# Tile 5 of the stick-breaking heads turned by VectorE and DRAM, with a newly planned instruction order

## The chip, the cores and the metric

The kernel runs on one core of a Trainium2 chip. The metric is device time in microseconds (us), the median of the runs shown, lower is better. PE is TensorE (matmul), PEld its weight load, DVE VectorE, ACT ScalarE, POOL GpSimd, SP SyncE, whose queue issues all DMA transfers.

## What is computed

One layer of a streaming encoder, for a prompt of 1024 rows and a sample of 32 rows, model width 1024, all in float32. Two groups of eight heads of 64 share one input projection: A is band attention with a clipped position bias, B is stick-breaking attention.

```python
qa, ka, va, ga, qb, kb, vb, gb = split(rmsnorm(h, g_pre) @ w_in)        # 8 x 512 columns

# A: each 64-row chunk reads itself and the 8 chunks before it
w = softmax(where(ok, qa @ ka.T * HEAD_DIM**-0.5 + bias[clip(k - q)], -1e30)); oa = w @ va

# B: strictly causal
z = qb @ kb.T * HEAD_DIM**-0.5
log_1m = where(causal, log_sigmoid(-z), 0)
after = cumsum(log_1m, reverse=True) - log_1m
w = where(causal, exp(log_sigmoid(z) + after), 0); ob = w @ vb

y = concat(oa * silu(ga), ob * silu(gb)) @ w_out
h = h + rmsnorm(y, g_post)
h = h + sigmoid(h @ w_ple_gate) * (p @ w_ple)
```

The keys and values are outputs too. The sample rows attend to cached keys and values.

## The kernel before

**Split operands.** Every float32 operand of a product is split in a rounded high part and the remainder, and three (or two) products of the parts are summed. So each turned tile costs a copy (high part, ACT) and a subtraction (low part, mostly DVE).

**The attention stages.** There are eight stages n = 0 to 7, for the head pairs A0, B0, A1, B1, A2, B2, A3, B3; each has two heads. While PE works on the scores and values of stage n, the projections of the pair of stage n + 1 are woven between (24 matmuls of 352 columns for each of three chunks and each of q, k, v); in the last stage these are the gates. A head has eight query tiles i of 128 rows. For each tile:

- `scores(i)`: score matmuls into up to two of three PSUM banks `S`. For B: DVE adds the mask on the diagonal block, ACT makes two sigmoids (of -z into `om`, of z into `be`), DVE's scan multiplies up from the right in `om`, POOL multiplies `be` by `om`. Tile i has i + 1 blocks of 128 columns in B, at most five in A.
- `weights_t(i)`: turns the weights, since the value product needs keys on the partitions. The usual way is by PE: transposes by 128x128 block into one of two PSUM banks `ptw`, four blocks to a bank, then ACT copies to `wTh` and DVE subtracts into `wTl`.
- `values(g)`: for each half g (tiles 0 to 3, 4 to 7) value matmuls into `PV`, ACT and DVE combine its halves, and a transfer stores `ot` to `o_dr`.

`om` and `be` are rings of 3076 and 3640 columns; a tile's room is taken again after its last use. A stage is followed by the next without a barrier.

**The way past PE.** Tiles named in `ROUND` go another way: A's tile 5, and B's tiles 4 and 6. Each group of `ROUND` goes by itself:

```python
for x, _, _ in done_with:
    y = slice(first[x], first[x] + cost(x))
    nc.vector.transpose(squares[:, y], w1[:, y.start * P:y.stop * P])
dr = scratch([P, m * P], f"swap{nm}_{i}")
dma(dr, w0[:, 0:m * P])
for c in range(4):
    x = dr[:, c * m * 32:(c + 1) * m * 32].rearrange("(g k) x -> k g x", k=32)
    dma(w1[32 * c:32 * c + 32].rearrange("k (g x) -> k g x", g=4), x)
```

DVE turns each 32x32 square in place of the block (from `be` to `om`), one transfer writes `om` to DRAM (`swapB`), four read it back with the squares in their turned places (to `be`), and then ACT copies to `wTh` and DVE subtracts into `wTl`, both from `be`.

**The order.** The program records all operations (one line, L490, issues them all, so rows of the profile are told apart by tile names), and `order()` lists them by a plan: a queue for each engine, durations from `cost()`, and a key by which the waiting operations of an engine are ranked. The key is the place of recording, plus an offset by engine and name of the written tile (`AHEAD_OF`). `RATES`, `SPACE_S`, `SPACE_T`, `SPACE_V`, `SUMS_STEP` and `SAMPLE_AT` set how attention, projections, the sums of weights and the sample's attention are woven when recorded. On the chip each engine runs its list in this order and waits on semaphores.

**After the attention.** The output product and the gate product (`o0P` to `o3P`, `g0P` to `g3P`) are by Strassen's seven products for blocks of 128 rows; tile 8, the sample, goes by itself. Rows of the hidden state (`h`) are normed, x is added by POOL, and they are stored to `h_dr`; the gate reads them back, turned by DVE (`lg`, `ug` from `ht`). Blocks of the gate's weights (`gB`, `gT`) are split meanwhile. `uu` is the gate's running sum.

Of the kernel before, what the change touches and what calls it, by code (L numbers as in the profile page):

```python
# [8 lines left out]
F32 = mybir.dt.float32  # L9
# [16 lines left out]
SCALE = HD ** -0.5  # L26
NT = 9
AHEAD_OF = {
    ('ACT', 'L'): 100, ('ACT', 'Qfs'): 50, ('ACT', 'stq'): 400, ('ACT', 'x'): -50,
# [3 lines left out]
}  # L33

ROUND = {"A": ((5,),), "B": ((4,),(6,))}
LAG_T = 2
LAG_V = 2
SPACE_S = {'A': 0.1, 'B': 0}  # L40
SPACE_T = {'A': 0.4, 'B': 0.4}
SPACE_V = {'A': 0.05, 'B': 0.0}
PARTS = 4
BEHIND = 2
RATES = (0.96, 0.86, 0.92, 1.0, 1.0, 0.86, 1.12, 0.86)
PLE_LAG = 4.0


# [224 lines left out]
class Recorder:  # L273


    def __init__(self):
        self.with_table, self.old_table = [], []
        self.ops, self.cls, self.low, self.closed, self.turns = [], 0, 0, [], []
        self.tensor = Engine(self, "PE", "tensor")
        self.vector = Engine(self, "DVE", "vector")  # L280
        self.scalar = Engine(self, "ACT", "scalar")
        self.gpsimd = Engine(self, "POOL", "gpsimd")
        self.sync = Engine(self, "SP", "sync")
# [26 lines left out]
    def node(self, eng, what, args, kw, after):  # L310
        o = Op()
        o.eng, o.what, o.args, o.kw, o.after = eng, what, args, kw, after
        o.key = (self.cls if eng == "PE" else self.low, len(self.ops))
        o.shared, o.table = False, None
        self.ops.append(o)
        return o

    def add(self, eng, what, args, kw):
        writes, reads = [], []
        method = what[1] if isinstance(what, tuple) else ""  # L320
        for i, a in enumerate(args):
            if isinstance(a, (View, Raw, Segments)):
                (writes if i == 0 or (method == "tensor_tensor_reduce" and i == 7) else reads).append(a)
        for k, a in kw.items():
            if isinstance(a, (View, Raw, Segments)):
                (writes if k in ("out", "accum_out") else reads).append(a)
        o = self.node(eng, what, args, kw, set())
        for mine, write in ((reads, False), (writes, True)):
            for v in mine:
                b = v.buf  # L330
                hit = False
                for other, box, wrote in b.uses:
                    if other is not o and (write or wrote) and all(p < y and x < q for (p, q), (x, y) in zip(v.box, box)):
                        o.after.add(other)
                        hit = True
                if b.pool is not None:
                    if not hit:
                        o.after.add(b.place)
                    b.pool.ops.append(o)
                b.uses.append((o, v.box, write))  # L340
        if method == "activation" and args[2] in (AF.Exp, AF.Sigmoid):

            o.table = args[2]
            if self.with_table and self.with_table[-1].table != o.table:
                self.old_table, self.with_table = self.with_table, []
            self.with_table.append(o)
            o.after.update(self.old_table)
        if eng != "PE" and writes:
            name = str(writes[0].buf.name)
            kind = (eng, name[:next((i for i, x in enumerate(name) if x.isdigit() or x in "AB_"), len(name))])  # L350
            o.key = (o.key[0], o.key[1] + AHEAD_OF.get(kind, 0))
        o.busy, o.late = self.cost(eng, method, args, kw, writes, reads)
        if eng == "SP":
            o.pieces = max(self.pieces(v) for v in args[0:2])
        o.shared = eng == "POOL"
        if eng == "DVE":
            sbuf = [v for v in reads if isinstance(v, (View, Segments)) and not v.buf.psum and v.free() > 4]
            o.shared = len(sbuf) > 1 or (method == "tensor_copy" and len(sbuf) == 1 and not writes[0].buf.psum)
# [9 lines left out]
    @staticmethod  # L368
    def cost(eng, method, args, kw, writes, reads):

        out = writes[0] if writes else None
        n = out.free() if isinstance(out, View) else 1
        psum = any(isinstance(v, (View, Segments)) and v.buf.psum for v in reads)
        if eng == "PE":
            if method == "transpose":
                return (109 if args[1].shape[0] > 64 else 62), 165
            return max(109.0, 2.5 + 0.449 * args[2].free()) * (1 if args[2].buf.dtype == F32R else 4), 165
        if eng == "ACT":
            return (165 if psum else 200) + 0.83 * n + (190 if "accum_out" in kw else 0), 0
        if eng == "DVE":  # L380
            if method == "tensor_tensor_scan":
                return 155 + 2.08 * n, 0
            if method == "tensor_copy" and not psum:
                return 155 + 0.53 * n, 0
            if method == "scalar_tensor_tensor":
                return 210 + 1.04 * n, 0
            return 155 + 1.04 * n + (83 if method == "tensor_tensor_reduce" else 0), 0
        if eng == "POOL":
            if method == "tensor_tensor":
                if n == 1:  # L390
                    return 400, 0
                return 190 + (1.77 if out.buf.dtype == F32 else 2.15) * n, 0
            if method == "tensor_scalar":
                return 255 + 0.86 * n, 0
            return 100 + 0.82 * n, 0
        size, run = 4, 0
        for v in (out, args[1]):
            if isinstance(v, View) and v.buf.pool is not None:
                size, run = 4 * v.shape[0] * v.free(), 4 * v.shape[-1]
        return ISSUE, max(size / DMA_RATE, size / run * (8.5 + 0.0365 * run) / 16)  # L400
# [95 lines left out]
def stream_step(  # L496
# [6 lines left out]
    rec = Recorder()  # L503
# [12 lines left out]
    def scratch(shape, name):  # L516
# [28 lines left out]
        out=maskb, in_=maskb, pattern=[[-1, P]], base=0, channel_multiplier=1,  # L545
# [4 lines left out]
    ksS = const.tile([P, 4, NS], F32, tag="ksS", name="ksS")  # L550
# [735 lines left out]
    for n in range(-1, 8):  # L1286
        a = len(order)
        if n < 7:
            ab, p = pairs[n + 1]
# [120 lines left out]
                sub(b[key], b["B11"], b[key], ALU.subtract)  # L1410
                dma(sum_dr[w][kt, 3], b[key])

    SUMS_STEP = {2: [8, 34], 4: [10, 28], 5: [8, 28], 6: [14, 28]}

    def with_sums(n, att, todo):
        out = list(att)
# [1 line left out]
            out.insert(SUMS_STEP[n][i], (0.0, lambda w=w, kt=kt: sum_weights(w, kt), None))  # L1418
        return out

    SAMPLE_AT = {2: [0, 10, 16, 23, 26, 27], 3: [4, 10, 15, 22, 27, 32], 6: [1, 10, 15, 22, 27, 32], 7: [1, 9, 15, 22, 23, 32]}

    def with_sample(n, att, steps):
        out = list(att)
# [15 lines left out]
    ple = Ple(True)  # L1440
# [56 lines left out]

    seq = attention_stream()
    for n in range(8):
        den = []  # L1500
        for j in range(*span[n + 1]):
            den += col_steps(j)
        att = seq[n, 0] + seq[n, 1]
        if pairs[n][1] % 2 == 1:
            att = with_sample(n, att, sample_attention(pairs[n][0], pairs[n][1] // 2))
        att = with_sums(n, att, SUMS_AT.get(n, ()))
        weave(n, att, den)
# [2 lines left out]


    rec.close(at_stack, at)
    fb = rec.pool(ctx, tc, name="fb", bufs=1)
    GP = fb.tile([P, D], F32, tag="GP", name="GP")
    L, R = HALF
# [17 lines left out]
    ple = Ple(False)  # L1533
# [62 lines left out]
    def fetch_T(src, dst, t):  # L1596

        if src is og_dr:
            for k0 in (0, 4):
                dma(dst[:, k0:k0 + 4, :], rows_T(og_dr, k0, t))  # L1600
            return
        t0, n = rows_of(t)


        h = fa.tile([P, D], F32, tag="hh", name=f"ht{t}", bufs=2)
        dma(h[:, 0:8 * n], h1_dr[t].rearrange("b (k g) c -> (b k) (g c)", k=32))
        squares = h[:, 0:8 * n].rearrange("p (g j m) -> p g m j", j=32, m=8)
        nc.vector.transpose(dst.rearrange("p m (k g) -> p g m k", k=32), squares)


    class Side:
# [187 lines left out]

    for m, (nm, src, group) in enumerate(sets):  # L1800
        last_set = m == len(sets) - 1
        state = [{}, {}]
        for n, prod in enumerate(ORDER):
            for pair, t in enumerate(group):
# [32 lines left out]
                for c, bank in zip(pieces, banks):  # L1837
                    multiply(bank[:, c], left, b, c)
                    if nm == "g" and prod == "P3":
                        uu = st["uu"]  # L1840
# [29 lines left out]
                else:  # L1870
                    uu = st.get("uu")
                    if prod in ("P2", "P4") and pair == 0:
                        name = f"cc{m}{prod}"
                        if m == 2 and prod == "P4":
                            cc = at2.tile([P, 2, 512], F32, tag="stg", name=name, bufs=3)
                        elif m == 3 and prod == "P2":
                            cc = at0.tile([P, 2, 512], F32, tag="L0", name=name)
# [78 lines left out]
```

## Time and profile before

| | |
|---|---|
| runs | 783.26, 783.63, 783.88 us; median 783.63 |
| profiled execution | 783.64 us, span 781.9 us |
| granted TensorE clock | 0.999 |
| busy, us | PE 769.8, PEld 711.2, DVE 602.9, ACT 528.4, POOL 471.7 |
| DMA | 154.71 MB, mean 198 GB/s |

A row of a group reads: line, engine, operation, written tile <- read tiles, shapes, count | busy us in all, mean ns of one | idle us of the engine before them, and what ended it. A busy PE is not PE at its peak: matmuls overlap, and their ends are modelled.

### The profile page before, as it was taken

To read this page: it belongs to the slowest core of one execution; us is meant where nothing else is said; L and a number is where in the kernel's file an instruction comes from. 1 tells how busy PE (TensorE), PEld (TensorE's weight loads), DVE (VectorE), ACT (ScalarE), POOL (GpSimd) and SP (SyncE) were. 2 spreads that over 40 slices of the span, in tenths; PEclk is the share of its full clock that TensorE was granted. 3 is DMA by queue.
4 is the path that set the end of the run, shared out by engine and by line. 5 is a ranking of instruction groups with operands and counts; after the bars stand their busy time and mean duration, and the time that the engine had idled before them with its cause. 6 is when DMAs were issued, how large, how long until landed. Compare 5 with 4: busy or idle time off the path is not lost.

```text
span 781.9 us, 14437 instructions
## 1 busy us (share of the span) xinstructions
PE 769.8 (98%) x4534; PEld 711.2 (91%) x4534; DVE 602.9 (77%) x1127; ACT 528.4 (68%) x1146; POOL 471.7 (60%) x551
## 2 busy tenths in 40 slices
PE   8999999999999999999999999999999999999997
PEld 6999999999999999999999999999998877877786
DVE  7827767888778888688988798888474687988965
ACT  5647775877786777787767777674347867685651
POOL 5636624574666446775966677575553438599533
PEclk9999999999999999999999999999999999999999
DMA  8657634557765638776757977775689856659754
GB/s 301 215 152 180 161 82 139 136 128 210 177 196 167 183 92 240 185 213 210 197 143 199 260 209 218 197 223 167 184 276 289 274 181 220 239 160 346 250 181 134
DMA packets 184542, 154.71 MB, mean 198 GB/s; under 512 B 64705, under 2 KB 150505, under 8 KB 184466
## 3 DMA queue, kind: packets, MB, share of 16 engines
q1 hardware_dynamic: 184466, 153.79, 66.8%
q8 instruction: 36, 0.59, 0.3%
q14 instruction: 40, 0.33, 0.1%
HBM read 94.97 MB, written 50.36 MB: 186 GB/s over the span
## 4 chain that ended last, share of the span: by engine, by line
PE 80%; POOL 7%; DVE 4%; DMA 3%; issue 3%; SPq 2%; ACT 1%; POOLq 0%; DVEq 0%; ACTq 0%
PE mm_gB L490 6%; PE mm_qB L490 6%; PE mm_qA L490 5%; PE mm_vA L490 5%; PE mm_kA L490 5%; PE mm_vB L490 5%; PE mm_kB L490 4%; PE PVB L490 4%; PE SB L490 4%; PE PVA L490 3%; PE SA L490 3%; PE ptwA L490 3%; PE o1P L490 3%; PE g2P L490 2%; PE o0P L490 2%
## 5 line engine op out<-in xcount | busy, mean ns | idle before, releaser
L490 POOL TENSOR_TENSOR be<-be,om 128x256 f32<-128x256 f32 (+8 forms) x66 | 83.5, 1269 | 82.1 <-DVE om L490 48.9
L490 DVE TENSOR_TENSOR_SCAN om<-om,SB 128x384 f32<-128x384 f32 (+5 forms) x96 | 92.6, 968 | 20.2 <-ACT be L490 11.1
L490 ACT ACTIVATE om<-SB 128x384 f32<-128x384 f32 (+5 forms) x96 | 46.6, 499 | 23.8 <-DVE SB L490 12.5
L490 POOL TENSOR_SCALAR be<-be,statA 128x640 f32<-128x640 f32 (+4 forms) x64 | 46.0, 727 | 25.8 <-DVE statA L490 22.2
L490 ACT ACTIVATE be<-SB 128x384 f32<-128x384 f32 (+5 forms) x96 | 46.3, 500 | 13.2 <-DVE om L490 6.6
L490 ACT ACTIVATE be<-om,statA 128x640 f32<-128x640 f32 (+4 forms) x64 | 44.4, 695 | 5.9 <-DVE statA L490 3.9
L490 DVE TENSOR_TENSOR wTl<-ptwA,wTh 128x512 fp32r<-128x512 f32 (+2 forms) x80 | 37.2, 482 | 12.5 <-ACT wTh L490 11.4
L490 ACT CAST wTh<-ptwA 128x512 fp32r<-128x512 f32 (+2 forms) x80 | 32.2, 425 | 20.4 <-PE ptwA L490 19.1
L490 ACT CAST wTh<-ptwB 128x512 fp32r<-128x512 f32 (+3 forms) x64 | 29.8, 488 | 15.4 <-PE ptwB L490 10.7
L490 DVE TENSOR_TENSOR wTl<-ptwB,wTh 128x512 fp32r<-128x512 f32 (+3 forms) x64 | 33.5, 542 | 5.3 <-ACT wTh L490 4.9
L490 PE MATMUL SB<-kdB,LB 128*128 128x384 f32 (+5 forms) x96 | 33.4, 353 | 0.4 <-DVE om L490 0.3
L490 PE MATMUL ptwA<-ident,be 128*128 128x128 f32 x200 | 33.2, 273 | 0.0
L490 DVE CUSTOM_DVE_ANT_0 om<-SA,biasA 128x320 f32<-128x320 f32 (+3 forms) x64 | 30.3, 482 | 3.6 <-PE SA L490 3.0
L490 PE MATMUL SB<-klB,LB 128*128 128x384 f32 (+5 forms) x96 | 32.5, 342 | 0.0
L490 PE MATMUL SA<-kdA,LA 128*128 128x320 f32 (+2 forms) x96 | 30.4, 320 | 0.1
L490 PE MATMUL ptwB<-ident,be 128*128 128x128 f32 x192 | 29.1, 274 | 1.3 <-POOL be L490 1.0
L490 DVE TENSOR_TENSOR wTl<-be,wTh 128x640 fp32r<-128x640 f32 (+1 forms) x24 | 29.1, 1211 | 1.0 <-ACT wTh L490 1.0
L490 PE MATMUL SA<-klA,LA 128*128 128x320 f32 (+2 forms) x96 | 29.9, 315 | 0.0
L490 POOL TENSOR_TENSOR gB<-gB,gB 128x256 f32<-128x256 f32 x32 | 26.0, 821 | 1.5 <-DMA gB<-in_w_ple_gate_dram 1.3
L490 PEld LDWEIGHTS ptwB<-ident,be 128*128 128x128 f32 x192 | 23.0, 140 | 3.1 <-POOL be L490 1.7
L490 POOL TENSOR_TENSOR klA<-stkA,kdA 64x1024 fp32r<-64x1024 f32 (+2 forms) x9 | 19.4, 2152 | 10.5 <-ACT kdA L490 10.2
L490 PEld LDWEIGHTS ptwA<-ident,be 128*128 128x128 f32 x200 | 24.8, 140 | 0.8
(696 smaller groups left out, 2667.5 us busy)
## 6 DMA issues: line engine op xcount, KB each, us to landing
oB<-in_w_out_dram SPq DMA_DIRECT2D x16, 256.0 KB, 3.6
sum_dro<-oB SPq DMA_DIRECT2D x16, 256.0 KB, 3.1
gB<-in_w_ple_gate_dram SPq DMA_DIRECT2D x16, 256.0 KB, 3.2
sum_drg<-gB SPq DMA_DIRECT2D x16, 256.0 KB, 2.3
x<-in_x_prompt_dram SPq DMA_DIRECT2D x16, 256.0 KB, 3.4
h_dr<-h SPq DMA_DIRECT2D x8, 512.0 KB, 3.6
ht<-h_dr SPq DMA_DIRECT2D x8, 512.0 KB, 4.4
raw<-sum_drg SPq DMA_DIRECT2D x16, 256.0 KB, 4.1
```

What stands on the lines that cost most here:

```text
L490: getattr(getattr(tc.nc, o.what[0]), o.what[1])(*args, **kw)
```

## The change

- `ROUND["B"]` gets a third group, tile 5. The six blocks of that tile are turned in all eight B heads by DVE and DRAM; 48 transposes on PE go.
- The plan's durations change: POOL's products from 190 + 1.77 n (2.15 n for split parts) to 200 + 1.9 n (2.3 n), the accumulating ACT pass from 190 to 80 more than a plain one, DVE's reducing pass from 83 more to 2% more, and the 1024 column transposes of `fetch_T` (strided 32x32 squares) to 2290 ns.
- A second table of offsets, `AHEAD_AT`, is added to the key by stage (0 the start, 1 to 8 the attention, 9 the passage, 10 to 13 the four Strassen sets), engine and tile; `AHEAD_OF` has new entries. The offsets now apply to PE too, and to operations that write DRAM (by the tile they read, as `to cc`).
- `RATES`, `SPACE_S`, `SPACE_T`, `SPACE_V`, `SUMS_STEP` and one place of `SAMPLE_AT` change.

```diff
 AHEAD_OF = {
-    ('ACT', 'L'): 100, ('ACT', 'Qfs'): 50, ('ACT', 'stq'): 400, ('ACT', 'x'): -50,
...
+    ('ACT', 'L'): 329, ('ACT', 'S'): -1196, ('ACT', 'be'): -16, ('ACT', 'kd'): 796,
...
+    ('SP', 'pp'): -611, ('SP', 'stv'): -823,
 }
+AHEAD_AT = {
+    (0, 'ACT', 'sq'): -249, (0, 'DVE', 'pleo'): -309, (1, 'ACT', 'stv'): 1111, (1, 'DVE', 'stat'): -309,
...
+    (12, 'ACT', 'wh'): -767, (12, 'DVE', 'lg'): 1498, (12, 'DVE', 'ug'): 1148, (12, 'SP', 'hh'): 123,
+    (12, 'SP', 'to cc'): 194,
+}
-ROUND = {"A": ((5,),), "B": ((4,),(6,))}
+ROUND = {"A": ((5,),), "B": ((4,), (5,), (6,))}
-SPACE_S = {'A': 0.1, 'B': 0}
-SPACE_T = {'A': 0.4, 'B': 0.4}
-SPACE_V = {'A': 0.05, 'B': 0.0}
+SPACE_S = {'A': 0.15, 'B': 0.05}
+SPACE_T = {'A': 0.35, 'B': 0.4}
+SPACE_V = {'A': 0, 'B': 0}
-RATES = (0.96, 0.86, 0.92, 1.0, 1.0, 0.86, 1.12, 0.86)
+RATES = (1.0, 0.84, 0.92, 0.94, 1.0, 0.88, 1.14, 1.0)
...
-        if eng != "PE" and writes:
-            name = str(writes[0].buf.name)
-            kind = (eng, name[:next((i for i, x in enumerate(name) if x.isdigit() or x in "AB_"), len(name))])
-            o.key = (o.key[0], o.key[1] + AHEAD_OF.get(kind, 0))
+        v = (writes or reads)[0].buf.name if writes or reads else ""
+        kind = eng, ("" if writes else "to ") + v[:next((i for i, x in enumerate(v) if x in "0123456789AB_"), len(v))]
+        n = o.key[2]
+        o.key = o.key[0], n + AHEAD_OF.get(kind, 0) + AHEAD_AT.get((self.stage, *kind), 0), n
...
-            return (165 if psum else 200) + 0.83 * n + (190 if "accum_out" in kw else 0), 0
+            return (165 if psum else 200) + 0.83 * n + (80 if "accum_out" in kw else 0), 0
...
-            return 155 + 1.04 * n + (83 if method == "tensor_tensor_reduce" else 0), 0
+            return (155 + 1.04 * n) * (1.02 if method == "tensor_tensor_reduce" else 1), 0
...
-                return 190 + (1.77 if out.buf.dtype == F32 else 2.15) * n, 0
+                return 200 + (1.9 if out.buf.dtype == F32 else 2.3) * n, 0
...
-    SUMS_STEP = {2: [8, 34], 4: [10, 28], 5: [8, 28], 6: [14, 28]}
+    SUMS_STEP = {2: [10, 31], 4: [10, 22], 5: [3, 30], 6: [8, 28]}
...
         nc.vector.transpose(dst.rearrange("p m (k g) -> p g m k", k=32), squares)
+        rec.ops[-1].busy = 2290.0
```

Stage numbers of `AHEAD_AT` are set by `rec.stage` as the operations are recorded. No other operation is added or taken away.

More of the change, by code (lines that the diff above doesn't have):

```diff
@@ L28 @@
 AHEAD_OF = {
-    ('ACT', 'L'): 100, ('ACT', 'Qfs'): 50, ('ACT', 'stq'): 400, ('ACT', 'x'): -50,
[3 rows of a table removed]
-}
-ROUND = {"A": ((5,),), "B": ((4,),(6,))}
+    ('ACT', 'L'): 329, ('ACT', 'S'): -1196, ('ACT', 'be'): -16, ('ACT', 'kd'): 796,
+    ('ACT', 'newh'): -56, ('ACT', 'oT'): -600, ('ACT', 'om'): -36, ('ACT', 'p'): -23,
+    ('ACT', 'v'): 51, ('DVE', 'Kl'): 1140, ('DVE', 'Vh'): -16, ('DVE', 'gT'): -158,
+    ('DVE', 'om'): -178, ('DVE', 'ot'): 166, ('DVE', 'uu'): -34, ('DVE', 'vt'): 131,
+    ('DVE', 'wl'): 758, ('DVE', 'wls'): 131, ('POOL', 'kl'): 934, ('POOL', 'wl'): 27,
@@ new lines @@
+    ('SP', 'GP'): 272, ('SP', 'Kcs'): -461, ('SP', 'be'): 17, ('SP', 'o'): 49,
+    ('SP', 'pp'): -611, ('SP', 'stv'): -823,
+}
+AHEAD_AT = {
+    (0, 'ACT', 'sq'): -249, (0, 'DVE', 'pleo'): -309, (1, 'ACT', 'stv'): 1111, (1, 'DVE', 'stat'): -309,
+    (1, 'PE', 'ptw'): 174, (2, 'ACT', 'be'): 54, (2, 'ACT', 'v'): 127, (2, 'ACT', 'wTh'): -885,
+    (2, 'ACT', 'wh'): -57, (2, 'DVE', 'S'): -238, (2, 'DVE', 'ot'): -112, (2, 'DVE', 'vx'): -293,
+    (3, 'ACT', 'Kh'): -162, (3, 'ACT', 'be'): 443, (3, 'ACT', 'ot'): -574, (3, 'ACT', 'stq'): 399,
+    (3, 'ACT', 'w'): 692, (3, 'ACT', 'wTh'): -1352, (3, 'DVE', 'Kcs'): -84, (3, 'DVE', 'S'): -1167,
+    (3, 'DVE', 'Vh'): 222, (3, 'DVE', 'w'): -332, (3, 'PE', 'PV'): 1076, (3, 'PE', 'Ss'): 1432,
+    (3, 'SP', 'kd'): -118, (3, 'SP', 'kl'): -63, (4, 'ACT', 'be'): 76, (4, 'ACT', 'om'): 38,
+    (4, 'DVE', 'S'): -1067, (4, 'DVE', 'vt'): -1007, (4, 'DVE', 'wTl'): 571, (5, 'ACT', 'stq'): -509,
+    (5, 'ACT', 'wh'): 1431, (5, 'DVE', 'stat'): 886, (5, 'DVE', 'vt'): -279, (5, 'POOL', 'om'): -449,
+    (6, 'ACT', 'be'): 27, (6, 'ACT', 'v'): 29, (6, 'ACT', 'wTh'): 103, (6, 'DVE', 'om'): 123,
+    (6, 'DVE', 'ot'): 37, (6, 'POOL', 'ksS'): 600, (6, 'POOL', 'om'): 364, (6, 'SP', 'be'): 463,
+    (7, 'ACT', 'newh'): 1036, (7, 'ACT', 'wTh'): -428, (7, 'DVE', 'L'): -198, (7, 'DVE', 'S'): 1202,
+    (7, 'DVE', 'Vl'): -1133, (7, 'DVE', 'kt'): 76, (7, 'DVE', 'om'): 204, (7, 'DVE', 'w'): -825,
+    (7, 'DVE', 'wTl'): -310, (7, 'PE', 'ptw'): 1440, (7, 'SP', 'bias'): -214, (7, 'SP', 'o'): 69,
+    (7, 'SP', 'swap'): -328, (8, 'ACT', 'sgg'): -941, (8, 'DVE', 'S'): -79, (8, 'DVE', 'Vl'): 272,
+    (8, 'DVE', 'om'): 183, (8, 'DVE', 'sgg'): -911, (8, 'POOL', 'sgg'): 256, (8, 'SP', 'Kcs'): 610,
[4 rows of a table added]
+}
@@ L276, in __init__ @@
     def __init__(self):
-        self.with_table, self.old_table = [], []
+        self.with_table, self.old_table, self.stage = [], [], 0
         self.ops, self.cls, self.low, self.closed, self.turns = [], 0, 0, [], []
@@ L312, in node @@
         o.eng, o.what, o.args, o.kw, o.after = eng, what, args, kw, after
-        o.key = (self.cls if eng == "PE" else self.low, len(self.ops))
+        o.key = (self.cls if eng == "PE" else self.low, len(self.ops), len(self.ops))
         o.shared, o.table = False, None
@@ L1419, in with_sums @@
         return out
-    SAMPLE_AT = {2: [0, 10, 16, 23, 26, 27], 3: [4, 10, 15, 22, 27, 32], 6: [1, 10, 15, 22, 27, 32], 7: [1, 9, 15, 22, 23, 32]}
+    SAMPLE_AT = {2: [0, 10, 16, 23, 26, 27], 3: [4, 10, 15, 22, 27, 32], 6: [1, 10, 15, 23, 27, 32], 7: [1, 9, 15, 22, 23, 32]}
     def with_sample(n, att, steps):
@@ L1499, in stream_step @@
     for n in range(8):
+        rec.stage = n + 1
         den = []
@@ L1512, in stream_step @@
     rec.close(at_stack, at)
+    rec.stage = 9
     fb = rec.pool(ctx, tc, name="fb", bufs=1)
@@ L1801, in stream_step @@
         last_set = m == len(sets) - 1
+        rec.stage = 10 + m
         state = [{}, {}]
```

5 rows, old and new, of tables (AHEAD_AT, AHEAD_OF) are left out of this document.

## The prediction

> **What bounds the kernel now.** I read the share of each engine first, then busy time by stage, then who TensorE (PE) waits for, then single matmuls.
>
> ```profile
> span 781.9 us, 14437 instructions
> PE 769.8 (98%) x4534; PEld 711.2 (91%) x4534; DVE 602.9 (77%) x1127; ACT 528.4 (68%) x1146; POOL 471.7 (60%) x551
> ```
>
> PE is busy in all but 12.1 us. The profiled execution took 783.64 us, so 1.74 us lie around its span; the median of the runs is 783.63, so the sum below can be read against the median as it stands. The changed part sits in the B heads. Four stages hold them; the columns are the stretch in us, its length, then busy us of PE, weight loads, DVE (VectorE), ACT (ScalarE), POOL (GpSimd), then clock, DMA share and GB/s:
>
> ```profile
> 110.00:165.00 55.00, 55.00 (x347) 53.34 (x346) 43.44 (x70) 39.67 (x92) 28.97 (x35) 1.00 0.43 114
> 224.00:304.00 80.00, 79.59 (x505) 76.24 (x503) 68.43 (x110) 57.28 (x129) 46.64 (x56) 1.00 0.62 175
> 342.00:406.00 64.00, 63.69 (x404) 61.56 (x404) 54.74 (x85) 46.77 (x107) 45.58 (x62) 1.00 0.66 194
> 462.00:550.00 88.00, 87.80 (x562) 85.69 (x561) 74.86 (x125) 55.98 (x130) 60.04 (x66) 1.00 0.71 201
> sum 287.00, PE 286.08 PEld 276.83 DVE 241.47 ACT 199.70 POOL 181.23; mean PE 71.52 PEld 69.21 DVE 60.37 ACT 49.93 POOL 45.31
> ```
>
> In 287 us of B stages PE is idle for 0.92 us: whatever PE work leaves these stages shortens them, as long as the other engines still deliver in time. DVE is next, 241.47 of 287, 84%. The idle time of PE lies elsewhere:
>
> ```profile
> 0.00:20.00 20.00, 16.98 (x85) 13.79 (x86) 14.21 (x21) 12.14 (x22) 11.52 (x25) 1.00 0.89 303
> 700.00:725.00 25.00, 23.08 (x99) 18.15 (x98) 21.32 (x35) 13.72 (x29) 21.86 (x18) 1.00 0.99 339
> 750.00:782.00 32.00, 26.96 (x129) 22.26 (x127) 16.73 (x28) 7.46 (x14) 9.05 (x8) 0.97 0.47 151
> ```
>
> 3.02 us at the start, 1.92 at the passage from the output projection to the gate, 5.04 at the end, where only the last tile's sigmoid, sums and store remain. That is 9.98 of 12.1; about 2.1 us are spread over the rest. The longest waits of PE by name:
>
> ```profile
> PE ptx L490 <- DVE be L490: 1.5, 2, 1.2
> PE g0P L490 <- DVE S2g L490: 1.0, 1, 1.0
> PE g1P L490 <- DVE uu L490: 1.0, 1, 1.0
> ```
>
> **What the change takes from PE.** Tile 5 of a B head has six 128x128 blocks, which PE turned by six transposes. Eight heads make 48, and the instruction order of the changed kernel has 4486 matmuls against 4534. Busy time overprices them, since matmuls overlap; the price is the distance from start to start:
>
> ```profile
> 458.01 0.60 PE L490 MATMUL ptwA<-ident,be 128*128 128x128 f32 x4
> 458.36 0.41 PE L490 MATMUL mm_vB<-hnh,wl_vB 128*128 128x352 f32 x1
> 458.61 0.60 PE L490 MATMUL ptwA<-ident,be 128*128 128x128 f32 x4
> 458.97 0.90 PE L490 MATMUL mm_vB<-hnh,wl_vB 128*128 128x352 f32 x4
> 459.70 0.64 PE L490 MATMUL mm_vB<-hnl,wh_vB 128*128 128x352 f32 x3
> ```
>
> ```profile
> 471.03 1.46 PE L490 MATMUL mm_gA<-hnh,wl_gA 128*128 128x352 f32 x8
> 472.32 0.65 PE L490 MATMUL mm_gA<-hnl,wh_gA 128*128 128x352 f32 x3
> ```
>
> Eight matmuls of 352 columns take 472.32 - 471.03 = 1.29 us, 0.161 each. From 458.01 to 459.70 stand eight transposes and five such matmuls: 1.69 - 5 x 0.161 = 0.885, so 0.111 us for a transpose. 48 x 0.111 = **5.3 us** off PE. (The A transposes of these rows have the shape and operands of the B ones.)
>
> **What it puts on the other engines.** The old way of tile 5 was, for each head, two PSUM evictions (512 and 256 columns) on ACT and DVE; the new way is that of tiles 4 and 6: a 32x32 transpose on DVE, one write to DRAM, four reads back, one copy on ACT, one subtraction on DVE. Tiles 4 and 6 have 640 and 896 columns, tile 5 has 768, the middle of both:
>
> ```profile
> L490 DVE TENSOR_TENSOR wTl<-ptwB,wTh 128x512 fp32r<-128x512 f32 x32 | 21.2, 677 | 3.8 <-ACT wTh L490 3.5 <-PE PVB L490 0.4
> L490 DVE TENSOR_TENSOR wTl<-ptwB,wTh 128x256 fp32r<-128x256 f32 x16 | 6.6, 411 | 0.3 <-ACT wTh L490 0.3
> L490 DVE TENSOR_TENSOR wTl<-be,wTh 128x640 fp32r<-128x640 f32 x16 | 17.9, 1121 | 0.6 <-ACT wTh L490 0.6
> L490 DVE TENSOR_TENSOR wTl<-be,wTh 128x896 fp32r<-128x896 f32 x8 | 11.1, 1391 | 0.4 <-ACT wTh L490 0.4
> L490 DVE STREAM_TRANSPOSE om<-be 128x640 f32<-128x640 f32 x16 | 13.3, 832 | 0.1
> L490 DVE STREAM_TRANSPOSE om<-be 128x896 f32<-128x896 f32 x8 | 8.8, 1105 | 0.7 <-POOL om L490 0.6
> L490 ACT CAST wTh<-ptwB 128x512 fp32r<-128x512 f32 x32 | 18.5, 594 | 14.7 <-PE ptwB L490 10.2 <-PE PVB L490 4.5
> L490 ACT CAST wTh<-be 128x896 fp32r<-128x896 f32 x8 | 7.6, 946 | 0.0
> ```
>
> DVE: + (832 + 1105) / 2 = 968, + (1121 + 1391) / 2 = 1256, - 677 - 411: 1.14 us a head, 9.1 us in all. The B stages go from 241.5 of 287 to 250.6 of 281.7, 89%: full, but not the bound. ACT: at least 0.594 goes and at most 0.946 comes for a head, so it gains under 0.35 us a head, 2.8 us at 70% busy: nothing on the path. SP gets five transfers a head, 40 in all:
>
> ```profile
> L490 SPq DMA_DIRECT2D be<-swapB x64: 318/430/1312, 130.9 to 544.0; - x64
> ```
>
> ```profile
> swapB<-om SPq DMA_DIRECT2D x8, 448.0 KB, 3.7
> be<-swapB SPq DMA_DIRECT2D x32, 112.0 KB, 2.7
> ```
>
> 40 x 0.43 = 17 us of a queue that is issued in order: the first read of each head waits there for the write to land (up to the 3.7 us of tile 6), and behind it stand the next weight slices, the o_dr stores and the two transfers that double the keys. Tiles 4 and 6 make the same wait twice a head already. The bytes, 8 x 2 x 384 KB, are 6.3 MB more in stages with a DMA share of 0.43 to 0.71: hidden.
>
> **Whether the longer way of tile 5 is covered.** Its way from the last score matmul to the value product, each step once:
>
> ```profile
> L490 DVE TENSOR_TENSOR SB<-SB,maskb 128x128 f32<-128x128 f32 x64 | 17.7, 290 | 8.3 <-PE SB L490 7.6
> L490 ACT ACTIVATE om<-SB 128x384 f32<-128x384 f32 x24 | 12.0, 499 | 4.9 <-DMA be<-swapB 2.0 <-PE SB L490 1.8 <-DVE SB L490 1.1
> L490 DVE TENSOR_TENSOR_SCAN om<-om,SB 128x384 f32<-128x384 f32 x24 | 23.2, 966 | 2.0 <-ACT be L490 1.4 <-ACT om L490 0.2
> L490 POOL TENSOR_TENSOR be<-be,om 128x768 f32<-128x768 f32 x8 | 12.4, 1551 | 13.9 <-DVE om L490 6.0 <-DMA swapB<-om 4.5 <-ACT be L490 3.4
> ```
>
> 0.29 + 2 x 0.50 + 2 x 0.97 + 1.55 + 0.97 + 3.7 + 2.7 + 0.95 + 1.26 = 14.4 us, with tile 6's own prices for the transfers and the ACT copy, which are upper bounds. In the new PE order I priced the matmuls between the last score of tile 5 and the first value product of its half by column (0.161 us for 352): 27.0 to 37.1 us in the eight heads, where the old order had 27.7 to 31.5. So 12.6 us or more are left for queues, and the expected cost on PE is nothing; without that cover it would be up to 14.4 us a head. The same count for tile 6, which already goes this way, gives 20.9 to 35.7 us against 21.3 to 34.1.
>
> **What the new order moves.** Every engine's order differs throughout, since offsets, spacings and rates are all new. I compared the distances on PE. From the scores of tile 7 of a B head to its transposes there are 7.2 to 13.5 us of PE work, 6.3 to 16.8 before. The tightest reuse of a score bank by B heads is 4.2 us against 4.0. So PE is not led closer to its producers; one place is tighter: between the two heads of A's last pair a transpose bank is asked for again after 0.6 us of PE work, while its eviction takes about 0.59 on ACT and 0.68 on DVE: 0.7 us of new wait or a little more. At the passage to the gate POOL now runs so:
>
> ```profile
> 697.50 4.22 POOL L490 TENSOR_TENSOR h<-h,x 128x512 f32<-128x512 f32 x3
> 701.69 2.54 POOL L490 TENSOR_TENSOR gT<-raw,gT 128x512 fp32r<-128x512 f32 x2
> 704.20 2.56 POOL L490 TENSOR_TENSOR h<-h,x 128x512 f32<-128x512 f32 x2
> ```
>
> The second half of row 2 is added behind two splits of gT; in the new order it comes ahead of them, so the row is stored about 2.5 us earlier. That store frees the room in which `uu` is made, and the 1.0 us that PE waited for `uu` should go; the 1.0 for `S2g` I leave. At the start tile 3's transposes come 16 matmuls earlier: I take zero, between the 1.5 us of the `ptx` waits gone and as much again. With that bank, and waits in the B stages that are 0.92 us now, I allow 0.7 of new waits, nearest to the row of the B stages; the ends are 0.9 gone and the 3.0 that PE loses at the start, where the other engines lead it. Sum: 783.64 - 5.3 - 1.0 + 0.7 = **778.0 us**.
>
> **The rivals.** *The new order also takes other waits away* (775.6): 12.1 us idle, less 5.04 at the end and the 1.0 counted, leave 6.1; two fifths of them, 2.4 us, give 775.6. For it: new offsets at stages 0 and 10 to 12. Against: part of the start is the wait for the first inputs, which no order changes.
>
> *The gain is given back as waits* (781 to 784): each B stage still has to finish its chain of scores, scans and products, and PE would idle where it used to transpose. For it: DVE goes to 89%. Against: projections of the next head fill PE, and the distances above did not shrink.
>
> [...]
>
> ```profile
> L490 DVE TENSOR_TENSOR wTl<-be,wTh x24: 781/1088/2702, 90.9 to 549.0; 128x640 fp32r<-128x640 f32 x16, 128x896 fp32r<-128x896 f32 x8
> ```
>
> The same work takes 0.78 to 2.70 us, and its mean is 1.75 ns a column (1121 / 640) against 1.32 out of PSUM (677 / 512): it is stretched by something. With eight more at the longest, 8 x 2.70, and the new transposes, 8 x 0.97, DVE gets 29 us, less 8.7 removed: 241.5 + 20.7 = 262 of 282 us, 93%, and POOL's products, which release PE's transposes, stand behind. If half of the new DVE time, 8.9 of 17.8 us at mean prices, reaches PE, the time is 783.64 - 5.3 + 8.9 = 787.2. It decides from 0.67 us a head, where 8 x 0.67 eats the 5.3.
>
> [...]
>
> That the change does not do what it says is excluded by the counts: 48 matmuls fewer, 8 DVE transposes and 40 transfers more.
>
> **How the numbers follow.** Forecast (776.5 to 780): 0.50. More waits gone: 0.17. Given back: 0.15, a third of it still under 782. Slower: 0.18. About 0.2%, 1.6 us, is what a measurement of this kernel can tell, so faster ends at 782.0: 0.50 + 0.17 + 0.05 = 0.72; same 0.08, slower 0.20. The range 775.0 to 785.0 leaves out most of the slower rival and the end of the better one, under 0.2.
>
> **What would show it.** Right: PE with 4486 matmuls, near 764 us busy, B stages still within 1 to 2 us of full, DVE 9 us more, no PE wait for `uu`. Wrong: PE idle over 15 us, with `SB` or `ptwB` waiting for DVE or POOL, `PVB` waiting for `wTl`, or `mm` products waiting for weight slices held up behind the reads of tile 5 in SP's queue.

## The result and the profile after

The changed kernel takes 776.63 us, the median of four runs (776.23 to 778.64), beside 783.75 for the kernel before in four runs (783.26 to 784.68): ratio 0.9913, 95% interval 0.9893 to 0.9932. The prediction had 778.0, with 776.5 to 780 as its forecast. The profiled execution took 776.69 us, of which 774.8 are its span.

The span and the busy time of each engine, after:

```profile
span 774.8 us, 14446 instructions
PE 764.6 (99%) x4486; PEld 706.7 (91%) x4486; DVE 600.0 (77%) x1127; ACT 526.7 (68%) x1138; POOL 473.1 (61%) x551
```

The span is 7.1 us shorter. PE's busy time gives 5.2 of it (769.8 to 764.6, with the 48 matmuls fewer), PE's idle time the other 1.9 (12.1 to 10.2). Where the idle time went is seen in the table by stretches, as in the prediction (us, length, then busy us of PE, weight loads, DVE, ACT, POOL, then clock, DMA share and GB/s). After:

```profile
0.00:20.00 20.00, 16.80 (x85) 14.06 (x86) 13.88 (x21) 11.73 (x21) 11.38 (x25) 1.00 0.90 300
20.00:400.00 380.00, 379.40 (x2430) 367.76 (x2429) 298.03 (x614) 273.47 (x611) 228.58 (x290) 1.00 0.65 182
400.00:450.00 50.00, 48.56 (x311) 45.84 (x310) 42.11 (x109) 38.37 (x88) 35.96 (x45) 1.00 0.87 239
450.00:700.00 250.00, 250.00 (x1354) 223.54 (x1354) 190.16 (x303) 167.09 (x352) 158.68 (x165) 1.00 0.76 232
700.00:725.00 25.00, 25.00 (x109) 19.89 (x108) 20.33 (x32) 12.98 (x27) 17.80 (x14) 1.00 0.91 324
750.00:774.80 24.80, 19.88 (x98) 16.50 (x96) 14.31 (x24) 6.08 (x11) 6.45 (x5) 0.98 0.39 126
```

and the three stretches of before that the prediction did not show:

```profile
20.00:400.00 380.00, 377.99 (x2426) 365.08 (x2426) 293.11 (x609) 273.36 (x609) 224.90 (x288) 1.00 0.62 171
400.00:450.00 50.00, 50.00 (x327) 48.69 (x326) 41.42 (x102) 37.04 (x85) 34.73 (x43) 1.00 0.76 210
450.00:700.00 250.00, 249.80 (x1369) 224.54 (x1368) 192.60 (x304) 166.19 (x357) 155.61 (x164) 1.00 0.71 217
```

The length less the PE column is PE's idle time. The passage to the gate (700 to 725) goes from 1.92 to nothing. Between 20 and 700 it is a trade: 2.01 becomes 0.60 before 400, nothing becomes 1.44 from 400 to 450, 0.20 becomes nothing after. The start goes from 3.02 to 3.20, and the end stays at 4.9. The longest waits of PE, after (us in total, times, longest):

```profile
PE idle L515 <- DVE newh L515: 1.3, 1, 1.3
PE ptx L515 <- DVE be L515: 1.2, 1, 1.2
PE ptwA L515 <- POOL qsS L515: 0.9, 1, 0.9
PE ple L515 <- ACT wph0True L515: 0.7, 1, 0.7
```

Both waits of the passage, for `S2g` and for `uu`, are gone. The new one, 0.9 at 438 us, lies between the heads of A's last pair. Last, the new operations and two groups of old work whose price moved; in the last row the three numbers are the shortest, the median and the longest subtraction in ns:

```profile
L515 DVE TENSOR_TENSOR wTl<-be,wTh 128x768 fp32r<-128x768 f32 x8 | 7.7, 968 | 0.3 <-ACT wTh L515 0.3
L515 DVE STREAM_TRANSPOSE om<-be 128x768 f32<-128x768 f32 x8 | 7.7, 960 | 0.7 <-POOL be L515 0.7
L515 DVE TENSOR_TENSOR v2B<-vtB,v2B 128x512 fp32r<-128x512 f32 x8 | 5.5, 709 | 0.2 <-ACT v2B L515 0.2
L515 DVE TENSOR_TENSOR oB<-woB,oB 128x512 fp32r<-128x512 f32 x8 | 6.5, 838 | 5.3 <-ACT oB L515 5.3
L515 DVE TENSOR_TENSOR wTl<-be,wTh x32: 798/1011/1842, 86.4 to 547.9; 128x640 fp32r<-128x640 f32 x16, 128x768 fp32r<-128x768 f32 x8, 128x896 fp32r<-128x896 f32 x8
```

and those two groups before:

```profile
L490 DVE TENSOR_TENSOR v2B<-vtB,v2B 128x512 fp32r<-128x512 f32 x8 | 8.2, 1050 | 2.0 <-ACT v2B L490 2.0
L490 DVE TENSOR_TENSOR oB<-woB,oB 128x512 fp32r<-128x512 f32 x8 | 8.5, 1100 | 2.7 <-ACT oB L490 2.7
```

The transpose costs what was predicted (960 against 968 ns), the subtraction less (968 against 1256). DVE is busy 2.9 us less than before, not 9.1 more.

### The profile page after: what moved, and what is told of

It reads as the page before. It is cut to its first block, busy times and chain, and to the rows that moved or that the text cites. A ratio compares the mean times of both kernels' runs of the same rounds, so it can differ in the third digit from the quotient of the medians.

```text
span 774.8 us, 14446 instructions
## 1 busy us (share of the span) xinstructions
PE 764.6 (99%) x4486; PEld 706.7 (91%) x4486; DVE 600.0 (77%) x1127; ACT 526.7 (68%) x1138; POOL 473.1 (61%) x551
## 4 chain that ended last, share of the span: by engine, by line
PE 89%; POOL 3%; DVE 3%; DMA 2%; ACT 1%; issue 1%; SPq 1%; POOLq 0%; ACTq 0%; DVEq 0%
PE mm_vB L515 6%; PE mm_gB L515 6%; PE mm_gA L515 6%; PE mm_qB L515 6%; PE mm_vA L515 5%; PE mm_kB L515 5%; PE mm_kA L515 5%; PE mm_qA L515 4%; PE PVB L515 4%; PE SB L515 4%; PE PVA L515 4%; PE SA L515 4%; PE ptwA L515 3%; PE o3P L515 3%; PE o1P L515 3%; PE g1P L515 3%
## 5 line engine op out<-in xcount | busy, mean ns | idle before, releaser
L515 ACT ACTIVATE be<-SB 128x384 f32<-128x384 f32 (+5 forms) x96 | 44.7, 497 | 7.8 <-DVE om L515 4.1
L515 DVE TENSOR_TENSOR wTl<-be,wTh 128x640 fp32r<-128x640 f32 (+2 forms) x32 | 35.7, 1123 | 6.0 <-ACT wTh L515 5.3
L515 DVE STREAM_TRANSPOSE om<-be 128x640 f32<-128x640 f32 (+2 forms) x32 | 29.8, 932 | 1.1 <-POOL be L515 0.9
L515 DVE TENSOR_TENSOR wTl<-ptwB,wTh 128x512 fp32r<-128x512 f32 (+3 forms) x48 | 25.4, 545 | 4.9 <-PE PVB L515 2.4
L515 ACT CAST wTh<-be 128x640 fp32r<-128x640 f32 (+2 forms) x32 | 25.6, 809 | 5.0 <-DMA be<-swapB 4.6
L515 ACT CAST wTh<-ptwB 128x512 fp32r<-128x512 f32 (+3 forms) x48 | 22.1, 485 | 8.6 <-PE ptwB L515 5.8
L515 POOL TENSOR_TENSOR gB<-gB,gB 128x256 f32<-128x256 f32 x32 | 26.5, 846 | 2.2 <-DMA kdB<-kdB 1.6
```

What stands on the lines that cost most here:

```text
L515: getattr(getattr(tc.nc, o.what[0]), o.what[1])(*args, **kw)
```

## The experiments

The theory behind the prediction: PE is the bound, 48 transposes are taken from it, and what replaces them is hidden. Four runs test that, a fifth follows up on DVE, and seven ask what the order of the instructions does. All times are medians; the ratio is to the kernel before, run on the same chip (783.2 to 783.5 us). Differences to after are between medians of different chips, on which before differs by up to 0.5 us.

**Tile 5 back on PE, the rest as after.** One more wait keeps the store's copy of one head behind its value products:

```diff
-ROUND = {"A": ((5,),), "B": ((4,), (5,), (6,))}
+ROUND = {"A": ((5,),), "B": ((4,), (6,))}
...
+                if nm == "A11":
+                    rec.ops[-1].after.add(stop)
```

> The changed kernel with B's tile 5 turned by PE again; all offsets, rates and durations of the plan stay (two ot copies of head A11 wait for their last value matmul, which leaves the changed kernel's order as it is). Theory (the gain is PE work plus the passage to the gate): 48 transposes come back at 0.111 us, PE busy 764.6 + 5.3 = 769.9, and the time 776.6 + 5.3 = 781.9, with about 1 us either way for new waits of a plan not made for it; the passage (700 to 725 us) stays without idle time. Rival (the gain is the new order, tile 5 is given back as waits): the time stays under 778.5.

Measured: 790.23 us (790.07 to 790.94), ratio 1.0091 [1.0074, 1.0107]. Both expectations are too low. The new plan without the new tile loses to the old kernel by 6.8 us. PE is busy 772.2 us, 2.4 more than before for the same 4534 matmuls, and idle 16.3; the chief wait is new, among A's gates (484 to 501 us):

```profile
PE mm_gA L515 <- DVE sggA L515: 5.3, 3, 3.7
```

**Tile 5 alone, in the kernel before.**

```diff
-ROUND = {"A": ((5,),), "B": ((4,),(6,))}
+ROUND = {"A": ((5,),), "B": ((4,), (5,), (6,))}
```

> The kernel before with tile 5 of B added to ROUND, nothing else. Theory: PE busy 769.8 - 5.3 = 764.5; time 783.7 - 5.3 = 778.4, from 777.5 to 780 with the waits that the old offsets leave, and the 1.9 us of PE idle at the passage to the gate stay. Rival (the gain is the new order): 782 to 785, with PE idle over 16 us.

Measured: 800.16 us (798.72 to 802.59), ratio 1.0219 [1.0198, 1.0239]. The theory missed by 22 us: with the old offsets the same move of the same tile loses 16.7 us. Its page:

```profile
span 796.8 us, 14400 instructions
PE 774.8 (97%) x4486; PEld 712.3 (89%) x4486; DVE 604.1 (76%) x1127; ACT 529.0 (66%) x1138; POOL 471.4 (59%) x551
```

PE is idle 22.0 us, and busy 10.2 us more than after for the same 4486 matmuls; the last section comes back to that. Both this run and the one with tile 5 back change more than the tile: `order()` plans anew from the operations, so each has an instruction order of its own. The waits are many and small, the largest these:

```profile
PE SB L490 <- DVE om L490: 3.1, 3, 2.6
PE ptwB L490 <- DVE wTl L490: 2.1, 1, 2.1
PE ptwA L490 <- POOL be L490: 1.5, 2, 1.0
```

**48 transposes more on PE, in the order of after.** As instructions are issued, the six transposes of tile 7 of each B head are issued twice:

```diff
+                    name = o.args[0].buf.name if o.eng == "PE" else ""
+                    if name.startswith("ptwB") and name[6:] in ("_7_0", "_7_4"):
+                        twice[name] = twice.get(name, 0) + 1
+                        if twice[name] <= (4 if name.endswith("0") else 2):
+                            getattr(getattr(tc.nc, o.what[0]), o.what[1])(*args, **kw)
```

> The changed kernel in its own order, but six transposes of tile 7 of each B head are done twice on PE (same result, 48 more). Theory (PE bounds the B stages, 0.111 us each): 776.6 + 5.3 = 781.9, PE busy up by 5.3, idle unchanged at 10.2. Rival (PE has slack at places where it waits for others, so its work is partly free): up by less than 3 us, with less idle time.

Measured: 780.67 us (780.22 to 780.79), ratio 0.9963 [0.995, 0.9976]; 4.0 us above after, 0.084 a transpose.

```profile
PE 768.7 (99%) x4534; PEld 711.2 (91%) x4534; DVE 602.1 (77%) x1127; ACT 526.4 (68%) x1138; POOL 471.9 (61%) x551
```

PE's busy time grows by 4.1 and the span by as much; PE's idle time stays at 10.2. So in this order PE's work sets the time, and 48 transposes are worth 4.0 us here against the 5.3 that were counted.

**Tile 5's DVE work twice, in the order of after.** Transpose and subtraction are each issued twice, 15.4 us at the prices of after:

```diff
+                    if o.eng == "DVE" and o.what[1] in ("transpose", "tensor_tensor") and o.args[1].buf.name[:3] == "beB" and o.args[1].buf.name[5:] == "_5":
+                        getattr(getattr(tc.nc, o.what[0]), o.what[1])(*args, **kw)
```

> The changed kernel in its own order, with the two DVE instructions of tile 5 in each B head (the 32x32 transpose, 0.96 us, and the subtraction, 0.97 us) done twice: 8 x 1.93 = 15.4 us more of DVE in the B stages. Theory (DVE of the new way is hidden): up by 0 to 1.5 us. [...]

Measured: 785.79 us (785.3 to 786.62), ratio 1.003 [1.0019, 1.0042]; 9.2 us above after, 0.60 for each us put on DVE (0.49 by DVE's busy total, which grew by 18.6). The theory falls on this point: more work on DVE in the B stages is not hidden. PE's idle time goes from 10.2 to 16.2 us and its busy time from 764.6 to 767.8. Waits of PE for DVE appear in several places:

```profile
PE PVB L515 <- DVE v2B L515: 1.7, 2, 1.2
...
PE SB L515 <- DVE om L515: 1.2, 2, 0.7
```

These are not waits for tile 5's own turned weights: no value product `PVB` waits for `wTl`, and for `wTh` only 0.3 us, as in after. What PE waits for is other work, which fits a delay in DVE's queue.

**Only the transposes twice.** The same edit for `transpose` alone, 7.7 us, which reads one SBUF tile: is it DVE's time as such that reaches PE, or only that of the subtraction, which reads two?

> The changed kernel in its own order, only the 32x32 transposes of tile 5 done twice: 8 x 0.96 = 7.7 us more of DVE, with one SBUF input each. Doing both DVE instructions twice had cost 9.2 us. If it is DVE's time that reaches PE: half of that, 4 to 5 us, so 780.5 to 782. [...]

Measured: 781.88 us (781.34 to 783.9), ratio 0.9987 [0.9976, 0.9998]; 5.2 us above after, 0.68 for each us. The subtractions add the other 4.0 for 7.7, 0.52 for each us. The ten runs spread over 2.6 us, so the two rates are not clearly apart, but 7.7 us of operations with one SBUF input put 5.2 us on the time: DVE's time is enough to explain it, and a second SBUF input is not needed.

**The plan's parts.** Tile 5 with the new durations in the kernel before, old offsets and rates (with equal keys ranked by place of recording):

```diff
-ROUND = {"A": ((5,),), "B": ((4,),(6,))}
+ROUND = {"A": ((5,),), "B": ((4,), (5,), (6,))}
...
-                return 190 + (1.77 if out.buf.dtype == F32 else 2.15) * n, 0
+                return 200 + (1.9 if out.buf.dtype == F32 else 2.3) * n, 0
...
```

> The kernel before with tile 5 of B added and the new durations of the plan (GpSimd products, strided squares, summing passes), with the old offsets, rates and spacings. If the longer durations are what makes room for tile 5: under 781, against 800.2 without them. If the offsets found for this very order are: 788 to 802, PE idle over 16 us.

Measured: 803.87 us (801.44 to 804.6), ratio 1.0258 [1.0239, 1.0276]. The more exact durations by themselves bring nothing of the gain. And after without its table of offsets by stage:

```diff
-        o.key = o.key[0], n + AHEAD_OF.get(kind, 0) + AHEAD_AT.get((self.stage, *kind), 0), n
+        o.key = o.key[0], n + AHEAD_OF.get(kind, 0) + 0, n
```

> The changed kernel without the table of offsets by stage (the general table, durations, rates and spacings stay). If the gain hangs on that table: 786 to 800, PE idle over 16 us, the work on PE as in the changed kernel (4486 matmuls). If it hangs on durations, rates and the general table: under 780.

Measured: 803.09 us (802.4 to 803.64), ratio 1.0253 [1.0237, 1.0268]. This table is worth 26.5 us in the changed kernel. With zero for only its stages 9 to 13, the passage and the Strassen sets:

```diff
-        o.key = o.key[0], n + AHEAD_OF.get(kind, 0) + AHEAD_AT.get((self.stage, *kind), 0), n
+        o.key = o.key[0], n + AHEAD_OF.get(kind, 0) + (AHEAD_AT.get((self.stage, *kind), 0) if self.stage < 9 else 0), n
```

> The changed kernel without the stage offsets of stages 9 to 13 (passage and Strassen sets); the attention's order stays but for single places. Theory (about 1.9 us of the gain are the passage to the gate): 778 to 780, PE idle between 690 and 730 us about 2 us, waits for uu or S2g back; the attention stages as in the changed kernel. Rival (that part came with the general table and the durations): under 777.3, no idle time there.

Measured: 781.38 us (780.3 to 784.79), ratio 0.9984 [0.9971, 0.9997]; 4.8 us by the medians, 3.7 by the spans of the profiled executions (778.5 against 774.8). That is above the 778 to 780 that the theory expected. PE's waits at the passage are back, though not all between 690 and 730 us, where PE is idle 0.66 us:

```profile
PE g0P L515 <- DVE A11g L515: 1.1, 1, 1.1
PE g1P L515 <- DVE wlA11g L515: 1.1, 1, 1.1
...
PE g L515 <- DVE uu L515: 0.8, 1, 0.8
```

If the two parts simply add, some 22 of the 26.5 us belong to the offsets of the start and the attention; no run sets these alone to zero.

**How much an order is worth that was not looked for.** The plan uses one duration of 60 ns for a semaphore (`SEM`). Changing it by 1 or 2 ns changes no work, only which of two waiting operations the plan ranks first; 993 of DVE's 1127 instructions keep their order in the first of these runs. In after:

```diff
-SEM = 60
+SEM = 61
```

> The changed kernel, with the same number moved by 1 ns; 993 of 1127 DVE instructions stay in their order. Theory (the new offsets fit one order only): 783 to 792, as much above 776.6 as the kernel before loses by the same step. Rival (the new durations and offsets make a robust plan): 776 to 778.5.

Measured: 784.89 us (783.35 to 787.25), ratio 1.0017 [1.0007, 1.0028]: 8.3 us above after for 1 ns in the plan. With 62:

> The changed kernel, the plan's semaphore time 62 instead of 60: a second draw of an order near to the tuned one, same work. The kernel before lost 4.9 and 12.7 us by steps of 1 ns, the changed kernel 8.3 by the first. Theory (offsets fit one order only, and what tile 5 takes from PE is still there between the untuned plans): 782 to 791, and the mean of both draws some 5 us under the mean of 788.3 and 796.2. Rival (robust): 776 to 778.5.

Measured: 796.6 us (796.24 to 797.79), ratio 1.0169 [1.0149, 1.0189]: 20 us above after, and above the 782 to 791 that the theory expected. In before, with 61 (equal keys ranked by place of recording, which alone leaves its order as it is):

> The kernel before, the plan's semaphore time 61 instead of 60 (equal keys are now ranked by the place of recording, which alone leaves the order before as it is); 982 of 1127 DVE instructions and 4234 of 4523 PE matmuls stay in their order. Theory (offsets fit one order only; the changed kernel lost 8.2 us by the same step): 788 to 797. Rival (the old plan is robust, and tile 5 alone costs its 17 us by itself): 782.5 to 785.5.

Measured: 788.31 us (787.93 to 791.02), ratio 1.0073 [1.0053, 1.0094]. With 59:

> The same with 59 instead of 60; 830 of 1127 DVE instructions stay in their order, so it goes farther from the old order. Theory: 790 to 802, as far as tile 5 alone (800.2). Rival: 782.5 to 785.5.

Measured: 796.15 us (794.49 to 797.33), ratio 1.0165 [1.0146, 1.0183]. All four neighbours are slower than the kernel that they come from: before by 4.9 and 12.7 us, after by 8.3 and 20.0. The two neighbours of before average 792.2, those of after 790.7. That leaves 1.5 us for tile 5 between orders that nobody looked for, where some 5 were expected, from two orders each and inside a spread of 12 us; the steps are not the same on both sides (+1 and -1 ns, +1 and +2 ns).

The profiled executions side by side, in us:

| kernel | span | PE busy | PE idle | DVE busy | clock |
|---|---|---|---|---|---|
| before | 781.9 | 769.8 | 12.1 | 602.9 | 0.999 |
| after | 774.8 | 764.6 | 10.2 | 600.0 | 0.999 |
| tile 5 back on PE | 788.5 | 772.2 | 16.3 | 604.3 | 0.997 |
| tile 5 alone | 796.8 | 774.8 | 22.0 | 604.1 | 0.991 |
| tile 5 and durations | 802.8 | 774.0 | 28.8 | 604.2 | 0.985 |
| no offsets by stage | 801.3 | 774.9 | 26.4 | 614.6 | 0.989 |
| after, 61 ns | 785.4 | 768.1 | 17.3 | 608.2 | 0.997 |
| after, 62 ns | 794.9 | 768.7 | 26.2 | 606.7 | 0.993 |
| before, 61 ns | 786.3 | 772.4 | 13.9 | 596.4 | 1.000 |
| before, 59 ns | 792.7 | 774.3 | 18.4 | 596.5 | 0.997 |

Each row is one execution, which can lie some us off the median of its runs (787.25 against 784.89 for after with 61 ns).

## Why the prediction came out, and which of its reasons did not hold

**The transposes (-5.3).** PE's busy time fell by 5.2 between the two traces, and adding 48 transposes to after added 4.0. The step held, its size perhaps 1 us too large: busy time also moves with the order (before with 61 ns has 2.6 us more of it for the same matmuls), so the 5.2 alone does not settle it.

**The passage (-1.0).** The wait for `uu` went. The one for `S2g`, which was left in, went too, so the term measured -1.9. This is the part of the result that the rival with more waits gone (775.6) has right; the time alone, 776.6, lies between it and the forecast. Setting the late offsets to zero brings `uu` back at 0.8 and two waits for DVE of 1.1, so the late offsets are what this term stands for.

**New waits (+0.7).** One came where it was expected, between the heads of A's last pair: 1.44 us from 400 to 450, of which 0.90 is a transpose held up. The view puts it down to POOL's `qsS`, but the times point to the eviction that was named:

```profile
436.73 0.75 ACT L515 CAST wTh<-ptwA 128x512 fp32r<-128x512 f32 x2 [1.49 <-PE ptwA L515]
437.35 0.89 DVE L515 TENSOR_TENSOR wTl<-ptwA,wTh 128x512 fp32r<-128x512 f32 x2 [1.92 <-ACT wTh L515]
437.94 0.23 POOL L515 TENSOR_SCALAR qsS<-stqB 128x32 f32<-128x32 f32 x1
438.16 0.14 PEld L515 LDWEIGHTS ptwA<-ident,be 128*128 128x128 f32 x1 [1.16 <-POOL qsS L515]
```

The weights of the transpose are loaded from 438.16, before `qsS` ends at 438.17. The first of the two subtractions, which empties the bank, takes 0.69 us and ends at 438.04; the copy ahead of it took 0.59. So this wait came as it was reasoned, with 0.90 us for 0.7. Against it 1.6 us of other waits between 20 and 700 went, and the start lost 0.2 more, so the term as a sum measured about 0. With the 0.9 of the passage, less the 0.1 by which the transposes gave less and the 0.15 by which the time around the span is longer, this is the 1.3 us between 778.0 and the profiled 776.7.

**DVE (+9.1 us, covered).** This is the step that failed. It has two halves, a size and a reason. The size was not met in this order. Tile 5's own edits are 7.7 + 7.7 us added, less eight subtractions of 512 and eight of 256 columns (8 x 0.677 and 8 x 0.411 by the prediction's rows, 8.7), so +6.7. DVE's total fell by 2.9 all the same, so its other operations are 9.6 us shorter in all; the largest pieces are subtractions that read two SBUF tiles, as in the groups of `v2B` (8.2 to 5.5 us) and `oB` (8.5 to 6.5). The price of such a subtraction changes with the order. The eight of tile 5 took 968 ns each in after, and in its neighbours with 61 and 62 ns and in tile 5 alone:

```profile
L515 DVE TENSOR_TENSOR wTl<-be,wTh 128x768 fp32r<-128x768 f32 x8 | 9.2, 1154 | 0.0
L515 DVE TENSOR_TENSOR wTl<-be,wTh 128x768 fp32r<-128x768 f32 x8 | 10.2, 1274 | 0.2 <-ACT wTh L515 0.2
L490 DVE TENSOR_TENSOR wTl<-be,wTh 128x768 fp32r<-128x768 f32 x8 | 12.4, 1556 | 0.7 <-ACT wTh L490 0.3 <-DMA be<-swapB 0.3
```

What stretches these subtractions no run shows. Between the neighbours of before (596.4 and 596.5 us of DVE) and those of after (608.2 and 606.7) DVE does grow by 11 us. So 9.1 was no bad price for orders that nobody looked for; the order of after made it vanish, and one trace's total, which differs by 6.5 us for the same work (596.4 to 602.9), does not measure it. The reason is where the step is wrong: "full, but not the bound". Doubling the work put 0.60 us on the time for each us on DVE, and the transposes alone 0.68. If that rate holds for the predicted 9.1 us, 5.5 would have come back and the sum would have been 783.5, so that the forecast came out is in part luck. The slower rival, 787.2 with half of DVE's new time reaching PE, had about the right sensitivity. Why it did not strike is not shown; that this order places the new work where PE does not meet it is a reading.

**"Distances on PE did not shrink, so the cover holds."** This reason was not enough. Distances on PE say what the order allows when every other engine delivers in time; they do not say when an engine's own queue reaches an operation. Tile 5 alone was expected near the sum and lost 16.7 us, and the same tile under two nearly equal plans lost 8.3 and 20.0 us to after. What is shown: the gain of 7.1 us exists in this order and in none of the others that were run, and the new plan without the tile loses 6.8 us to before. The two belong together; neither was an improvement alone.

**What stays open.** Whether 48 transposes less are still worth their 4 to 5 us between two equally well searched orders: the neighbours scatter by 12 us, too much to tell. That the offsets were searched for this exact set of work is an inference from all neighbours being slower; no run shows how they were found. No run points to a version that beats after.

## What to carry to other kernels

With PE 99% busy, work put on it in an unchanged order cost 0.084 us a transpose here, three quarters of the start-to-start distance of 0.111 us read from a trace; but "hidden" must be tested for the engine that receives it, by issuing its new work twice in the same order. Where a static order is planned from durations and offsets, compare a change with neighbours of both plans (1 ns more or less in one duration) before giving the change, or its offsets, the credit. A change of work without a newly fitted order can lose more, here 17 us, than the work itself can gain.

## What the runs showed of the hardware

Some gaps of PE cost more than their length here. PE's busy time for the same 4486 matmuls was 764.6 us in after and 774.0 to 774.9 in the three slowest orders with tile 5. In the run with tile 5 and the new durations, five stretches of 4 us each (columns as above; the clock is the third from the end) around the longest wait of PE:

```profile
412.00:416.00 4.00, 4.00 (x27) 3.92 (x25) 3.93 (x7) 1.65 (x5) 4.00 (x5) 1.00 0.74 263
416.00:420.00 4.00, 1.48 (x10) 1.19 (x8) 3.59 (x6) 3.97 (x6) 3.84 (x3) 0.95 0.62 157
420.00:424.00 4.00, 2.45 (x7) 2.19 (x8) 3.90 (x7) 2.11 (x6) 2.51 (x2) 0.50 0.94 258
424.00:428.00 4.00, 4.00 (x21) 3.91 (x20) 1.47 (x5) 1.67 (x6) 4.00 (x6) 0.70 0.67 207
428.00:432.00 4.00, 4.00 (x29) 3.96 (x28) 3.25 (x9) 2.46 (x4) 0.71 (x2) 1.00 0.71 197
```

and the matmul after that wait, with products of the same projection before and behind it (each with the row that follows):

```profile
412.76 1.45 PE L490 MATMUL mm_kB<-hnh,wh_kB 128*128 128x352 f32 x8
414.05 1.45 PE L490 MATMUL mm_kB<-hnh,wl_kB 128*128 128x352 f32 x8
...
421.55 0.66 PE L490 MATMUL mm_kB<-hnh,wh_kB 128*128 128x352 f32 x1 [4.07 <-ACT stkB L490]
...
424.06 1.67 PE L490 MATMUL mm_kB<-hnh,wh_kB 128*128 128x352 f32 x5
425.53 0.47 PE L490 MATMUL SA<-kdA,LA 128*128 128x320 f32 x1
```

PE idles 4.07 us, until 421.55, and the clock is 0.50 and 0.70 in the two stretches from 420 and 1.00 again from 428: 21 matmuls in the 4 us from 424, all busy, against 27 before the gap. From start to start a product of 352 columns takes 0.161 us before the gap (8 in 1.29) and 0.294 from 424.06 (5 in 1.47). Shorter gaps went ahead of such a fall too. In the run with tile 5 alone a wait of 2.07 us, until 391.78, was followed by a clock of 0.70 and 0.50 in the next two stretches of 2 us, and two shorter waits by the same fall:

```profile
451.64 0.76 PE L490 MATMUL ptwA<-ident,be 128*128 128x128 f32 x5 [0.97 <-POOL be L490]
453.07 0.52 PE L490 MATMUL SsA<-Kh0sA,QhsA 128*128 128x272 f32 x2 [0.67 <-ACT QhsA L490]
```

```profile
450.00:452.00 2.00, 1.03 (x8) 0.74 (x7) 0.48 (x3) 1.75 (x4) 0.97 (x3) 1.00 1.10 199
452.00:454.00 2.00, 1.29 (x9) 0.83 (x8) 1.69 (x4) 1.27 (x4) 1.91 (x3) 1.00 0.61 194
454.00:456.00 2.00, 1.95 (x9) 1.75 (x10) 1.58 (x6) 0.51 (x3) 1.33 (x3) 0.56 0.81 235
456.00:458.00 2.00, 1.90 (x7) 1.34 (x7) 1.19 (x6) 0.70 (x2) 0.00 (x0) 0.50 0.78 235
```

1.68 us of idle time within 4 us went ahead of this fall, while 1.44 us within 6 us in after (436 to 442) did not bring one (its clock is 1.00). Between the two waits PE did only five transposes. The mean clock of the whole run is 0.985 in the one with the most idle time and 0.999 in after. The first of these is busy 9.4 us longer on PE than after for the same 4486 matmuls (774.0 against 764.6), so by these numbers the clock is a part of why orders that lose a few waits lose more than the waits.
